# Scaling the second projections' outputs on ScalarE and adding them on GpSimd in a two-layer diffusion backbone

## The chip, the core and the metric

The kernel runs on one core of a Trainium2 chip. Its metric is the device time of one execution in microseconds (us), as the median of several runs. The engines are called by their names or, in rows of the profile, by short ones: PE is TensorE (PEld its weight loads), DVE VectorE, ACT ScalarE, POOL GpSimd, SP SyncE. Matmuls write to PSUM, which the kernel uses as eight banks of 512 float32 columns; everything else that is computed lives in SBUF. GpSimd does not appear in the kernel as a reader of PSUM: what it adds must first be in SBUF.

## The reference

512 latent tokens (`x`) and 256 context tokens (`ctx`) of width 1024 pass two layers. Each layer has three sub-layers: a SwiGLU feed-forward of inner width 2816 that counts half, a mixer (a short gated convolution in the first layer, attention in the second), and another half feed-forward. Every sub-layer has an RMSNorm, a shift and a scale, and a gate on its output, all three made from the conditioning vectors:

```python
h = norm_modulate(x_lat, norm_g[i, 0], m_lat[:, 0, 0], m_lat[:, 0, 1])
x_lat = x_lat + MACARON_WEIGHT * m_lat[:, 0, 2] * swiglu(h, ffn_w_in[i, 0], ffn_w_out[i, 0])

def swiglu(h, w_in, w_out):
    gate, up = jnp.split(h @ w_in, 2, axis=-1)
    return (jax.nn.silu(gate) * up) @ w_out
```

The vectors `m_lat` and `m_ctx` are `silu(c) @ ada_w + ada_b` for the latent and the context tokens. The context is carried as far as the attention reads it. The output is the latent stream after a last RMSNorm. What the change touches is the second product, `... @ w_out`, its gate and its addition to the stream.

## The kernel before

**Layout.** The stream of both kinds of tokens is one SBUF tile, `x_all`, of 8 chunks of 128 features with 768 tokens each: columns 0 to 511 latent, 512 to 767 context. Weights come by DMA as float32 (`raw`, five buffers) and are split into a high and a low half (`split`, lines 189 and 190): ScalarE rounds to the high one, VectorE subtracts for the low one. A product is then three matmuls (`mm3`, lines 861 to 863: high by high, high by low, low by high). Split weights go to eight tiles called `w`, filled ahead of TensorE; a tile is free again when TensorE has used it.

**Sub-layers.** They are named by layer and place: f00 (first feed-forward of the first layer), c01 (convolution), f02, f10, the attention, f12. In a feed-forward, `products` makes the first projection for 22 chunks of 128 inner features. The first two or three chunks are made directly, the others by seven half-size products M1 to M7 (`PRODUCTS`), whose operands are sums of quarters of the weights (lines 373 and 382, VectorE) and of the activations. Each product has a bank of PSUM under the tags A (three banks), C (three), B (one); ScalarE and VectorE take the results out (lines 1135 to 1212).

**Parts.** As soon as the chunks of a part are made, `out_steps` runs the second projection for them: `FFN_PARTS` is (2, 4, 4, 4, 4, 4), so a feed-forward has six parts, the first of two chunks, the others of four; the convolution has two. A part loops over the eight output chunks three at a time (3, 3, 2) and, for each, over the two token groups: 512 latent columns, then 256 context columns. A group takes three banks from A and C (`out_banks`), 12 matmuls of a bank in a part of four chunks. Then its eviction, line 929: VectorE reads the bank, multiplies it by the gate `gat` (a column of a tile) and adds the piece of the stream, in place. The last part of a sub-layer goes other ways: `out_close` (line 998) in f00, c01 and f02, `out_last` (line 1606) in f12, and in f10 `out_steps` itself with `after` set, which squares and norms the stream at once. The attention's output and f12 have one token group alone.

**Order.** TensorE's and SyncE's instructions keep the program's order. VectorE's, ScalarE's and GpSimd's are put in order by a scheduler that works with costs of its own; on the chip every engine works its queue in that order. In some stretches (the opening, the turn from one sub-layer to the next) the program's order holds for VectorE and ScalarE too.

**Work in the background.** The conditioning products run on VectorE in the shadow of the matmuls: `ada_step` (line 530) multiplies a 128 x 512 tile of `ada_w`, called `aw`, by `silu_row` and sums it, once for the latent and once for the context vector. `bg` and `bg_run` pace the steps over the products and the parts. The tiles `aw` are loaded by GpSimd's queue (`ada_next`, line 509) into four buffers in f00, two in c01, five in f02 and f10; each step asks for the load of the tile that many steps ahead, whose buffer that same step has just read.

**Small tiles.** The pool `tmp` has four tiles with the tag "t" of 512 columns, used in turn for squares, roots and the convolution's mixed rows; in the parts that the change touches they stand mostly unused.

Of the kernel before, what the change touches and what calls it, by code (L numbers as in the profile page):

```python
# [10 lines left out]
F32 = mybir.dt.float32  # L11
F32R = mybir.dt.float32r
BF16 = mybir.dt.bfloat16
AF = mybir.ActivationFunctionType
ALU = mybir.AluOpType
# [3 lines left out]
P = 128  # L19
# [4 lines left out]
NL = 512  # L24
# [54 lines left out]
def segments(off, n):  # L79

    out = []
    if off < NL:
        out.append((LAT, off, min(off + n, NL) - off))
    if off + n > NL:
        out.append((CTX, max(off, NL), off + n - max(off, NL)))
    return out
# [43 lines left out]
def backbone(ctx: ExitStack, tc: tile.TileContext, a: dict, out: bass.AP):  # L130
    nc = tc.nc
    act, dve, pe = nc.scalar, nc.vector, nc.tensor
# [3 lines left out]
    tmp = ctx.enter_context(tc.tile_pool(name="tmp", bufs=4))  # L136
    wp = ctx.enter_context(tc.tile_pool(name="wp", bufs=3))

    def ctile(name, shape, dt=F32):
        return const.tile(shape, dt, name=name, tag=name)  # L140
# [13 lines left out]
    def ptile(name, shape=(P, 512)):  # L154
        pool, tag = bank[name]
        return pool.tile(list(shape), F32, name=f"ps_{name}", tag=tag)
# [25 lines left out]
    gat = ctile("gat", [P, KC, 2])  # L182
# [108 lines left out]
    def w_get(most=1 << 30):  # L291
        w_fill(max(most, state["used"] + 1 - state["next"]))
        where, dst = ready[state["used"]]
        ready[state["used"]] = None
        state["used"] += 1
        taken.append(where)
        return dst
# [3 lines left out]
    def w_ahead(n):  # L301

        return w_get(max(0, state["used"] + 1 + n - state["next"]))

    def w_done():

        for where in taken:
            if where is None:
                state["open"] -= 1
            elif where[0] == "slot":  # L310
                state["extra"] -= 1
        taken.clear()
# [188 lines left out]
    ada_chunks, ada_loaded, ahead = [], {}, {}  # L501
    silu_row = {}

    def ada_next(n):

        if n < ahead["limit"]:
            t, kh, j = ada_chunks[n]
            w = ada_loaded[n] = ahead["pool"].tile([P, 512], F32, name=f"aw{t}_{kh}_{j}", tag="aw", bufs=ahead["depth"])
            nc.gpsimd.dma_start(w, a["ada_t"][t, kh, j])  # L509
# [12 lines left out]
    def ada_step(n, i, hm, nv):  # L522

        t, kh, j = ada_chunks[n]
        w = ada_loaded.pop(n)
        col = 4 * (hm % 2) + j
        for v in range(nv):
            total = mods[i][:, hm // 2, col, v : v + 1]
            junk = ptile("S")
            ins = dve.tensor_tensor_reduce(out=junk, in0=w, in1=silu_row[kh][:, v, :], scale=1.0, scalar=total if kh else ada_b[:, i, hm // 2, col : col + 1], op0=ALU.mult, op1=ALU.add, accum_out=total)  # L530
            tc.keep_in_program_order(ins)
        ada_next(n + ahead["depth"])
        if kh and j == 3:
            ada_done.add((i, hm))

    def ada_list():


        tasks = [(i, hm) for i in range(2) for hm in range(18) if i or hm > 5]
        at = 0  # L540
        for key, end in ADA_BY.items():
            steps = []
            for kh in range(2):
                steps += [lambda kh=kh: silu_load(kh)] + [rest] * 3
                for t in range(at, end):
                    i, hm = tasks[t]
                    for j in range(4):
                        steps.append(lambda n=len(ada_chunks), i=i, hm=hm: ada_step(n, i, hm, mod_groups(i, hm // 2)))
                        ada_chunks.append((t, kh, j))
            ada_tasks.extend((at, go) for go in steps)  # L550
            at = end
# [23 lines left out]
    def bg_run(share):  # L575
        if pace["n"] < pace["first"] or pace["done"] == pace["steps"]:
            return
        pace["used"] += share
        due = min(pace["steps"], int(np.ceil(pace["steps"] * pace["used"] / pace["room"] - 1e-6)))
        while pace["done"] < due:  # L580
            ada_tasks.pop(0)[1]()
            pace["done"] += 1
# [14 lines left out]
    def xs(m, off, n):  # L597
        return x_all[:, m, off : off + n]

    def sq_add(m, grp):  # L600
        off, n = grp
        if m == 0 and off == 0:
            ssq[:] = [stage["ssq"]()]
        if m == 0:
            act.activation(ssq[0][:, off : off + n], xs(m, off, n), AF.Square)
        else:
            sq_sum(sq_of(m, grp), grp)
# [11 lines left out]
    def preload_ln_exp():  # L619
        tc.keep_in_program_order(act.preload_act_table_set(LN_EXP))  # L620
# [39 lines left out]
    def norm_parts(grp):  # L660
        off, n = grp
        return parts_of(ssq[0][:, off : off + n], n, D)
# [62 lines left out]
    def in_order():  # L725

        region.append(ExitStack())
        region[0].enter_context(tc.manual_schedule(engines=BOOT_ORDERED))

    def free_order():  # L730
        region.pop().close()
# [128 lines left out]
    def mm3(ps, wh, wl, xh, xl, first, last, **kw):  # L860
        pe.matmul(ps, wh, xh, start=first, stop=False, **kw)  # L861
        pe.matmul(ps, wh, xl, start=False, stop=False, **kw)  # L862
        pe.matmul(ps, wl, xh, start=False, stop=last, **kw)  # L863
# [45 lines left out]
    def out_steps(groups, passes, gh, gl, npart, after, alloc, width, scarce=0):  # L909

        def run(grp, ms, units, major, tags=None):
            off, n = grp
            ps = [ptile(t) for t in tags] if tags else alloc(grp, len(ms))
            todo = [(f, u) for f in range(npart) for u in range(len(ms))] if major else [(f, u) for u in range(len(ms)) for f in range(npart)]
            for q, (f, u) in enumerate(todo):
                wh, wl = units[u]  # L920
                mm3(ps[u][:, :n], wh[:, f, :], wl[:, f, :], gh[f][:, off : off + n], gl[f][:, off : off + n], f == 0, f == npart - 1)
                if q % npart == npart - 1:
                    bg_run(OUT_SHARE * n / NT)
            if gates:
                gates.pop()()
            for m, p in zip(ms, ps):
                for v, o, w in segments(off, n):
                    x = xs(m, o, w)
                    dve.scalar_tensor_tensor(out=x, in0=p[:, o - off : o - off + w], scalar=gat[:, m, v : v + 1], in1=x, op0=ALU.mult, op1=ALU.add)  # L929

        held = []
        major = width == 3
        for m0 in range(0, KC, width):
            ms = range(m0, min(m0 + width, KC))
            units = [w_ahead(scarce) if scarce else w_get() for _ in ms]
            if after:
                run(passes[0], ms, units, major)
                held.append((ms, units))
                for m in ms:
                    sq_add(m, passes[0])  # L940
                if m0 < KC // 2 <= m0 + width:
                    preload_ln_exp()
                if ms[-1] < 6:
                    w_done()
                yield
            else:
                for grp in groups:
                    run(grp, ms, units, major)
                    major = False
                    yield  # L950
                w_done()
            major = False
        if after:
            in_order()
            steps = iter(after(passes[0], norm_parts(passes[0])))
            flat = [(m, u) for ms, units in held for m, u in zip(ms, units)]
            n2 = 1 if width == 3 else 2
            behind = PASS_STEPS[n2]
            for j in range(0, KC, n2):
                ms, units = zip(*flat[j : j + n2])  # L960
                run(passes[1], ms, units, False, LAST_BANKS[j : j + n2] if n2 == 1 else None)
                for what, n in behind.get(j, ()):
                    if what == "norm":
                        for _ in range(n):
                            for step in [next(steps, None)]:
                                if step:
                                    step()
                    else:
                        for m in n:
                            sq_add(m, passes[1])  # L970
            for step in steps:
                step()
            w_done()
            held_tiles.clear()
            pending.extend(after(passes[1], norm_parts(passes[1])))
            free_order()
# [724 lines left out]
    with tc.tile_pool(name="apool", bufs=1) as apool, tc.tile_pool(name="g0", bufs=1) as gp, tc.tile_pool(name="qp", bufs=1) as qp, psum(A=3, B=1, C=3, S=1):  # L1701
# [24 lines left out]
        with tc.tile_pool(name="boot", bufs=1) as bp, aw_pool():  # L1726
            in_order()
            op = opening(0, 0)
# [71 lines left out]
            op1 = opening(0, 1)  # L1800
# [94 lines left out]
```

## Time and profile before

| what | us |
|---|---|
| median of 3 runs | 2407.13 |
| lowest and highest run | 2406.97, 2408.5 |
| span of the profiled execution | 2405.2 |

The span goes from the first to the last instruction of one execution taken by the profiler; the runs' times are of other executions. A group's row gives its line, engine, operation, what it writes and reads, the shapes (partitions by elements) and the count, then busy time and the mean of one in ns, then how long the engine sat idle just before these instructions and who ended that. A row of stretches gives the stretch, its length, busy time and number of instructions of each engine in turn, the granted TensorE clock (1.00 is full), the busy share of the DMA engines and GB/s. A row of waits says who waited for whom: total, times, longest. A row of the timeline begins with start and duration. A busy matmul is one in flight, and neighbours overlap, so the step from one start to the next tells the pace.

### The profile page before, as it was taken

The numbers are of one execution on the slowest core, as the hardware profiler recorded it, in microseconds if no ns is written. First come the engines' busy times: TensorE is split into PE (matmuls) and PEld (weight loads), VectorE is DVE, ScalarE is ACT, GpSimd is POOL, SyncE is SP. The second block draws the span as 40 slices with busy tenths as digits, with TensorE's granted clock in tenths as the row PEclk, the third lists the DMA queues.
The fourth block names the chain that finished last, engine by engine and source line by source line (L and its number), as shares of the span: only waits on it lengthen the run. The fifth ranks groups of instructions, "written<-read, shape, count | busy, mean of one in ns | idle before, by whom it ended". The sixth has DMA issues, their size and how long they took to land.

```text
span 2405.2 us, 37639 instructions
## 1 busy us (share of the span) xinstructions
PE 2383.8 (99%) x14303; PEld 2258.6 (94%) x14303; DVE 2033.0 (85%) x4018; ACT 1164.8 (48%) x2198; POOL 135.2 (6%) x256
## 2 busy tenths in 40 slices
PE   8999999999999999999999999999999999999998
PEld 6999999999999999999999999999998889999998
DVE  6989989978988888888887988888778987987787
ACT  5634334355535653433435543343355776555555
POOL 0001111100000001000000001101100000000000
PEclk9999999999999999999999999999999999999999
DMA  9234444430334123323432144443441101133331
GB/s 334 87 112 137 130 126 129 131 115 27 106 106 132 33 69 115 127 93 119 126 100 73 49 124 126 146 136 122 141 131 45 53 10 58 67 110 102 106 106 62
DMA packets 93062, 253.71 MB, mean 105 GB/s; under 512 B 10320, under 2 KB 18640, under 8 KB 92880
## 3 DMA queue, kind: packets, MB, share of 16 engines
q1 hardware_dynamic: 71984, 183.65, 23.5%
q0 software_dynamic: 20352, 67.12, 9.4%
q8 instruction: 112, 1.84, 0.3%
q14 instruction: 70, 0.57, 0.1%
q10 hardware_dynamic: 544, 0.52, 0.1%
HBM read 249.16 MB, written 2.10 MB: 104 GB/s over the span
## 4 chain that ended last, share of the span: by engine, by line
PE 92%; DVE 3%; ACT 2%; DMA 1%; issue 1%; SPq 0%; DVEq 0%; ACTq 0%
PE ps_A L861 16%; PE ps_A L862 16%; PE ps_A L863 16%; PE ps_C L862 11%; PE ps_C L861 11%; PE ps_C L863 11%; PE ps_B L863 3%; PE ps_B L861 3%; PE ps_B L862 3%; PE ps_T L1542 1%; DMA ada<-in_ada_w 1%; ACT pr L1525 0%; DMA raw<-in_ffn_w_in 0%; DVE w L190 0%; PE ps_O L861 0%
## 5 line engine op out<-in xcount | busy, mean ns | idle before, releaser
L189 ACT ACTIVATE w<-raw 128x512 fp32r<-128x512 f32 (+1 forms) x862 | 522.4, 619 | 721.0 <-PE ps_A L863 229.7
L190 DVE TENSOR_TENSOR w<-raw,w 128x512 fp32r<-128x512 f32 (+1 forms) x862 | 574.3, 679 | 119.7 <-ACT w L189 105.8
L509 POOL DMA_DIRECT2D aw<-in_ada_t x240 | 129.1, 538 | 1374.8 <-DVE mods L530 973.9
L373 DVE TENSOR_TENSOR raw<-raw,raw 128x512 f32<-128x512 f32 x264 | 181.5, 689 | 9.0 <-DMA raw<-in_ffn_w_in 4.9
L862 PE MATMUL ps_C<-gl,w 128*128 128x512 f32 (+1 forms) x548 | 188.5, 344 | 0.0
L861 PE MATMUL ps_C<-gh,w 128*128 128x512 f32 (+1 forms) x548 | 188.4, 344 | 0.0
L863 PE MATMUL ps_C<-gh,w 128*128 128x512 f32 (+1 forms) x548 | 188.2, 343 | 0.0
L861 PE MATMUL ps_A<-gh,w 128*128 128x512 f32 (+1 forms) x540 | 185.8, 344 | 0.6 <-DVE x L929 0.6
L862 PE MATMUL ps_A<-gl,w 128*128 128x512 f32 (+1 forms) x540 | 185.7, 344 | 0.0
L863 PE MATMUL ps_A<-gh,w 128*128 128x512 f32 (+1 forms) x540 | 185.5, 344 | 0.0
L530 DVE CUSTOM_DVE_ANT_0 ps_S<-aw,silu_row,packed 128x512 f32<-128x512 f32 x208 | 156.9, 754 | 2.4 <-DMA aw<-in_ada_t 1.0
L530 DVE CUSTOM_DVE_ANT_0 ps_S<-aw,silu_row,mods 128x512 f32<-128x512 f32 x208 | 156.8, 754 | 1.0
L929 DVE SCALAR_TENSOR_TENSOR x<-ps_C,gat,x 128x512 f32<-128x512 f32 (+1 forms) x158 | 99.5, 631 | 43.1 <-PE ps_C L863 42.7
L861 PE MATMUL ps_A<-tB11h,w 128*128 128x384 f32 (+1 forms) x400 | 130.8, 327 | 0.2 <-ACT tB11h L785 0.2
L862 PE MATMUL ps_A<-tB11l,w 128*128 128x384 f32 (+1 forms) x400 | 130.3, 326 | 0.2 <-DVE tB11l L786 0.2
L863 PE MATMUL ps_A<-tB11h,w 128*128 128x384 f32 (+1 forms) x400 | 130.4, 326 | 0.0
L862 PE MATMUL ps_C<-tB22l,w 128*128 128x384 f32 (+2 forms) x376 | 121.8, 324 | 0.0
L863 PE MATMUL ps_C<-tB22h,w 128*128 128x384 f32 (+2 forms) x376 | 121.7, 324 | 0.0
L861 PE MATMUL ps_C<-tB22h,w 128*128 128x384 f32 (+2 forms) x376 | 121.5, 323 | 0.0
L929 DVE SCALAR_TENSOR_TENSOR x<-ps_A,gat,x 128x512 f32<-128x512 f32 (+1 forms) x162 | 101.8, 637 | 17.0 <-PE ps_A L863 16.7
L863 PEld LDWEIGHTS ps_C<-gh,w 128*128 128x128 f32 x548 | 103.9, 190 | 12.3
L861 PEld LDWEIGHTS ps_A<-gh,w 128*128 128x128 f32 x540 | 102.4, 190 | 14.0 <-issue 1.0
(486 smaller groups left out, 6946.0 us busy)
## 6 DMA issues: line engine op xcount, KB each, us to landing
raw<-in_ffn_w_in SPq DMA_DIRECT2D x170, 512.0 KB, 3.7
aw<-in_ada_t POOLq DMA_DIRECT2D x240, 256.0 KB, 3.0
raw<-in_ffn_w_out SPq DMA_DIRECT2D x80, 512.0 KB, 4.1
raw<-in_conv_w_in SPq DMA_DIRECT2D x24, 512.0 KB, 3.7
ada<-in_ada_w SPq DMA_DIRECT2D x28, 256.0 KB, 5.7
raw<-in_attn_w_qkv SPq DMA_DIRECT2D x12, 512.0 KB, 4.9
raw<-in_ada_w SPq DMA_DIRECT2D x8, 512.0 KB, 6.8
silu_row<-in_crow POOLq DMA_DIRECT2D x8, 512.0 KB, 4.2
```

The costliest lines, as they stand in the source:

```text
L189: hi = act.activation(dsth, src, AF.Copy)
L190: lo = dve.tensor_tensor(out=dstl, in0=src, in1=dsth.bitcast(F32), op=ALU.subtract)
L373: dve.tensor_tensor(out=quad(o), in0=quad(x), in1=quad(y), op=ALU.subtract)
L509: nc.gpsimd.dma_start(w, a["ada_t"][t, kh, j])
L530: ins = dve.tensor_tensor_reduce(out=junk, in0=w, in1=silu_row[kh][:, v, :], scale=1.0, scalar=total if kh else ada_b[:, i, hm // 2, col : ...
L861: pe.matmul(ps, wh, xh, start=first, stop=False, **kw)
L862: pe.matmul(ps, wh, xl, start=False, stop=False, **kw)
L863: pe.matmul(ps, wl, xh, start=False, stop=last, **kw)
L929: dve.scalar_tensor_tensor(out=x, in0=p[:, o - off : o - off + w], scalar=gat[:, m, v : v + 1], in1=x, op0=ALU.mult, op1=ALU.add)
L1542: pe.transpose(pt[:, c, :], pr[:, (c0 + c) * P : (c0 + c + 1) * P], ident)
```

## The change

Two places. In `out_steps`, an eviction of a part that is neither a sub-layer's last (`after` unset) nor of one token group alone is now two instructions: ScalarE's activation Copy reads the bank, multiplies by the gate and writes a `tmp` tile "t" named `oy`; GpSimd adds that tile to the stream, in place. The bank is free when ScalarE has read it, the tile when GpSimd has added it. Other evictions stay as they were. In `ada_step`, the load that a step asks for is that of the step before it: after step n it is tile n - 1 + depth, not n + depth; the first step of a sub-layer asks for none. The buffer that a load fills is the one that step n - 1 has read.

```diff
@@ ada_step
-        ada_next(n + ahead["depth"])
+        if n > ahead["start"]:
+            ada_next(n - 1 + ahead["depth"])
@@ out_steps, run
                 for v, o, w in segments(off, n):
                     x = xs(m, o, w)
-                    dve.scalar_tensor_tensor(out=x, in0=p[:, o - off : o - off + w], scalar=gat[:, m, v : v + 1], in1=x, op0=ALU.mult, op1=ALU.add)
+                    if after or len(groups) == 1:
+                        dve.scalar_tensor_tensor(out=x, in0=p[:, o - off : o - off + w], scalar=gat[:, m, v : v + 1], in1=x, op0=ALU.mult, op1=ALU.add)
+                    else:
+                        y = tmp.tile([P, NL], F32, name="oy", tag="t")[:, :w]
+                        act.activation(y, p[:, o - off : o - off + w], AF.Copy, scale=gat[:, m, v : v + 1])
+                        nc.gpsimd.tensor_tensor(out=x, in0=x, in1=y, op=ALU.add)
```

## The prediction

> **What bounds the kernel now.** I read the page first, then the busy time by stretches, then the list of what TensorE waited for, and last the timeline, because a busy TensorE need not be one at its peak. The first row is the span; in the second each engine has its busy time, its share and its number of instructions.
>
> ```profile
> span 2405.2 us, 37639 instructions
> PE 2383.8 (99%) x14303; PEld 2258.6 (94%) x14303; DVE 2033.0 (85%) x4018; ACT 1164.8 (48%) x2198; POOL 135.2 (6%) x256
> ```
>
> The parts that the change touches end between 76 and 1790 us. The next fence cuts the span there; behind the length of a stretch stand the busy times of TensorE, its weight loads, VectorE, ScalarE and GpSimd. Below is all that TensorE waited for in the middle stretch.
>
> ```profile
> 0.00:76.00 76.00, 69.54 (x381) 50.54 (x382) 52.66 (x106) 48.60 (x86) 3.54 (x11) 1.00 0.84 296
> 76.00:1790.00 1714.00, 1713.19 (x9808) 1655.93 (x9807) 1473.56 (x2928) 748.42 (x1371) 130.68 (x243) 1.00 0.35 109
> 1790.00:2405.20 615.20, 601.04 (x4117) 552.10 (x4116) 506.80 (x986) 367.80 (x742) 0.98 (x2) 1.00 0.22 72
> ```
>
> ```profile
> PE ps_A L861 <- DVE x L929: 0.6, 1, 0.6
> ```
>
> TensorE is idle for 1714.00 - 1713.19 = 0.81 us of the 1714 us, 0.6 of it in one wait for an eviction of the very line that is changed. The clock granted is 1.00 throughout. It remains that matmuls might run closer together than they do. The timeline shows them under a busy VectorE (an ada step, 170.15 to 170.90) and under an idle one (the last row: idle for 1.82 us before 936.64).
>
> ```profile
> 170.15 0.75 DVE L530 CUSTOM_DVE_ANT_0 ps_S<-aw,silu_row,packed 128x512 f32<-128x512 f32 x1
> 170.63 0.39 PE L862 MATMUL ps_C<-gl,w 128*128 128x512 f32 x1
> 170.86 0.39 PE L863 MATMUL ps_C<-gh,w 128*128 128x512 f32 x1
> ...
> 935.31 0.39 PE L862 MATMUL ps_C<-gl,w 128*128 128x512 f32 x1
> 935.53 0.39 PE L863 MATMUL ps_C<-gh,w 128*128 128x512 f32 x1
> ...
> 936.64 0.75 DVE L929 SCALAR_TENSOR_TENSOR x<-ps_C,gat,x 128x512 f32<-128x512 f32 x1 [1.82 <-PE ps_C L863]
> ```
>
> The step from one 512-column matmul to the next is 0.23 us in the first case and 0.22 in the second. Relieving VectorE does not quicken it. So the kernel is bound by TensorE's own stream, and what the change can win in its stretch is 0.81 us.
>
> **The change part by part.** The evictions in question are those of line 929:
>
> ```profile
> L929 DVE SCALAR_TENSOR_TENSOR x<-ps_A,gat,x 128x512 f32<-128x512 f32 x95 | 69.8, 748 | 15.6 <-PE ps_A L863 15.4
> L929 DVE SCALAR_TENSOR_TENSOR x<-ps_C,gat,x 128x512 f32<-128x512 f32 x89 | 66.6, 748 | 42.9 <-PE ps_C L863 42.7
> L929 DVE SCALAR_TENSOR_TENSOR x<-ps_C,gat,x 128x256 f32<-128x256 f32 x69 | 32.9, 480 | 0.2
> L929 DVE SCALAR_TENSOR_TENSOR x<-ps_A,gat,x 128x256 f32<-128x256 f32 x67 | 32.2, 480 | 1.3 <-PE ps_A L863 1.3
> ```
>
> Of these 184 + 136, 56 + 8 stay: those with one token group alone (40 in f12, 8 in the attention) and the last part of f10 (8 + 8). 128 of each form move: 16 parts (five of f00, f02 and f10, one of c01) with 8 + 8 each.
>
> VectorE loses 8 x (0.748 + 0.480) = 9.8 us a part, 157 us in all. ScalarE's and GpSimd's new instructions are not in the trace; these rows are nearest:
>
> ```profile
> L1135 ACT ACTIVATE g<-ps_A 128x256 f32<-128x256 f32 x20 | 7.6, 381 | 8.8 <-PE ps_A L863 8.8
> L1398 ACT ACTIVATE hs<-ps_A 128x512 f32<-128x512 f32 x6 | 3.5, 588 | 0.1
> L189 ACT ACTIVATE gh<-g 128x384 fp32r<-128x384 f32 x118 | 61.9, 524 | 44.8 <-DVE g L1212 36.8 <-DVE g L1204 8.0
> L1289 ACT ACTIVATE cy<-u,packed 128x384 f32<-128x384 f32 x8 | 4.9, 612 | 2.1 <-DVE u L1308 2.0
> masks.py:199 POOL TENSOR_SCALAR_AFFINE_SELECT ident<-ident 128x128 f32<-128x128 f32 x1 | 0.8, 772 | 0.1
> masks.py:199 POOL TENSOR_SCALAR_AFFINE_SELECT identb<-identb 128x128 f32<-128x128 f32 x1 | 0.3, 292 | 0.1
> L190 DVE TENSOR_TENSOR w<-raw,w 128x512 fp32r<-128x512 f32 x830 | 562.2, 689 | 119.7 <-ACT w L189 105.8
> ```
>
> ScalarE reads 512 columns of PSUM in 0.588 us and 256 in 0.381; a scale that is a column of a tile costs 0.612 - 0.524 = 0.088 more (third and fourth row). So 8 x (0.676 + 0.469) = 9.2 us a part, at least 7.8 without that surcharge, at most the 9.8 that VectorE needs now. GpSimd adds two SBUF tensors. Below it stands VectorE's own two-input instruction, 0.689 us for 512 columns, half of that for 256; above it the slower of GpSimd's two selects, 0.772 for 128 columns, which makes 3.1 and 1.5. I take the faster select (0.292), 1.17 and 0.58, because it is nearer to the VectorE row for the same work and the same operation stands in both selects. That is 8 x 1.75 = 14.0 us a part (8.3 to 37), beside the DMA issues. Now the cover, in parts of f00, f00's products, f02's first part, and another part of f02:
>
> ```profile
> 832.00:857.00 25.00, 24.89 (x143) 22.64 (x142) 24.81 (x45) 10.96 (x20) 0.00 (x0) 1.00 0.22 74
> 915.00:951.00 36.00, 36.00 (x209) 32.21 (x208) 32.16 (x71) 6.59 (x12) 4.84 (x9) 1.00 0.37 110
> 154.00:188.00 34.00, 34.00 (x198) 30.34 (x198) 33.23 (x78) 5.93 (x10) 5.92 (x11) 1.00 0.40 113
> 188.00:246.00 58.00, 58.00 (x333) 57.87 (x332) 52.56 (x109) 29.09 (x54) 5.91 (x11) 1.00 0.44 144
> ```
>
> ScalarE goes from 5.93 to 15.1 of 34 us, and in the short part from 10.96 to 20.2 of 25. GpSimd goes from 5.92 to 19.9 of 34. VectorE falls from 33.23 to 23.4. None is full, so all of this lies beside TensorE's work: I cost it at nothing. A new wait is ScalarE's, for the end of a group's matmuls; behind it in ScalarE's order stand splits of weights. What they are early by shows in what ScalarE waits for between 915 and 951 us:
>
> ```profile
> ACT w L189 <- PE ps_C L863: 12.0, 5, 7.2
> ACT w L189 <- PE ps_A L863: 6.6, 2, 5.8
> ```
>
> It waits up to 7.2 us for TensorE to give a weight tile back: all eight tiles are filled ahead, so a split that comes some us later finds its cover. Another new wait is for one of the four tmp tiles "t", which GpSimd frees. GpSimd works in order, and an add can stand behind an ada load that waits for VectorE:
>
> ```profile
> POOL aw L509 <- DVE mods L530: 23.5, 8, 9.4
> ```
>
> That is of 154 to 188 us; the longest of eight waits is 9.4 us. Four tiles hold an extra group of three, and a bank is asked for again one group pair later: 36 matmuls of 512 columns at 0.23 us and 36 of 256, at half of that, 12.4 us. So a delay of 9.4 us ends before the bank is wanted. Cost nothing; a delay 1 us beyond that in each of 16 parts would make 16 us, 2422.5.
>
> The load itself is moved one step back in the program, but the buffer that it fills is given free by the same step as before, so VectorE's wait for it need not change.
>
> ```profile
> aw<-in_ada_t POOLq DMA_DIRECT2D x240, 256.0 KB, 3.0
> ```
>
> Where adds hold the queue, a load lands late by their time, and VectorE waits up to 3.0 us. Only c01, with two buffers, is near that, and its weights are filled ahead too. Nothing again.
>
> The sum: the 0.6 us wait on line 929 goes, since that eviction stands behind VectorE's other work no longer; what is late next there is a split or ScalarE's own eviction, and the other 0.2 us of idle time stay. 2405.2 - 0.6 = 2404.6 us of span. The median of the runs, 2407.13, is 1.9 us above the profiled span, so 2406.5.
>
> **The rivals.**
>
> First, slower: GpSimd falls behind in the three parts of two chunks (f00, f02, f10). There the evictions come fastest, sixteen from 840.06 to 855.33, or 15.3 us:
>
> ```profile
> 840.06 0.74 DVE L929 SCALAR_TENSOR_TENSOR x<-ps_C,gat,x 128x512 f32<-128x512 f32 x1
> ...
> 855.33 0.48 DVE L929 SCALAR_TENSOR_TENSOR x<-ps_C,gat,x 128x256 f32<-128x256 f32 x1
> ```
>
> My 14.0 us just fits. If every add also waits out one VectorE instruction (0.689 us), an add takes 0.875 + 0.689 = 1.56 us and the part 25.0: GpSimd is 9.7 us late, the four tiles hold 4 x 1.56 = 6.2, and ScalarE, and then a bank, is held up to 3.5 us. Three parts give 10.5 us: 2417. It decides from where sixteen adds less four exceed 15.3 us, 1.28 us an add. For it: VectorE is busy 24.81 of 25 us there. Against it: the same stretch loses VectorE's evictions, and the idle group of banks may hold those 3.5 us.
>
> Second, slower: VectorE becomes the bound in f00. If it stands still during each add, a part and its products cost it 33.23 + 52.56 - 9.8 + 14.0 = 90.0 of 92 us. That fits; from 16 us of adds a part it does not. At 1.3 times my price (18.2) it lacks 2.2 us in each of four such rounds, 9 us: 2415.5. For it: most of VectorE's work there (ada steps, splits) reads two SBUF tensors. No row of this trace shows an add of GpSimd beside VectorE. The Trainium skill ("SBUF — State Buffer", section "Who interferes with whom") says that a VectorE instruction with two SBUF inputs and a GpSimd instruction that reads SBUF lock each other out, whichever begins first; that speaks against this change, and by it this rival and the one above both have their mechanism, at the prices given.
>
> Third, faster by more than a measurement can tell from no change (0.2%, 4.8 us): the changed queues shift the order of other work too, and the third stretch has 615.2 - 601.04 = 14.2 us of idle TensorE. A third of it gone would give 2402. Nothing in the change touches that stretch; the same shift could as well cost some.
>
> **How the numbers follow.** The forecast has 0.72: TensorE's stretch is full and every new instruction has cover. First rival 0.11, second 0.08, the longer wait in GpSimd's queue 0.03, third 0.06. Hence faster 0.06, same 0.72, slower 0.22. The time is the forecast's, 2406.5. Its own range is 2404 to 2410. The range for 8 in 10 reaches down to 2403.5, some 3 us for shifts of order, and up to 2416, over the second rival and most of the way to the first; about 0.15 is left out.
>
> **What would show it.** Line 929 with 64 instead of 320 instructions on VectorE; 256 new ones on ScalarE near 0.68 and 0.47 us, 256 on GpSimd near 1.17 and 0.58. TensorE between 76 and 1790 us idle for under 2 us, with its matmuls at the same steps. VectorE's busy time near 1876 us if nothing locks it; longer means of lines 190, 373 or 530 would show the lock. I am wrong if TensorE's waits name the new lines (ScalarE's eviction, or through it GpSimd's add) or splits of weights for several us in all, first at 90 to 110, 840 to 857 and 1352 to 1369 us.

## The result, and the profile after

The changed kernel takes 2480.81 us (median of 4 runs, 2478.99 to 2482.47) against 2407.05 for the kernel before on the same chip: ratio 1.0307, 95% interval 1.0295 to 1.032, so 74 us slower. The prediction said 2406.5, no change that could be measured.

The page of the changed kernel, its span and its engines' busy times (busy time, share of the span, number of instructions):

```profile
span 2479.8 us, 38129 instructions
PE 2408.4 (97%) x14303; PEld 2272.8 (92%) x14303; DVE 2122.0 (86%) x3762; ACT 1287.1 (52%) x2454; POOL 430.4 (17%) x512
```

The span grew by 2479.8 - 2405.2 = 74.6 us. TensorE has the same 14303 matmuls, yet is busy for 2408.4 - 2383.8 = 24.6 us longer: they ran slower. The other 50.0 us are idle time of TensorE. VectorE gave away 256 of its instructions, yet its busy time rose from 2033.0 to 2122.0 us.

What TensorE waited for, the first five rows (total, times, longest):

```profile
PE ps_C L862 <- ACT oy L934: 26.2, 7, 5.7
PE ps_A L862 <- DVE c L1152: 13.6, 11, 2.6
PE ps_A L862 <- ACT g L1149: 4.4, 2, 2.2
PE ps_C L484 <- DMA ada<-in_ada_w: 4.3, 1, 4.3
PE ps_A L863 <- DVE tT2l L190: 3.9, 1, 3.9
```

Up to line 531 both kernels number their lines alike; from there to the eviction this kernel's lines are those of before plus one, behind it plus six. The longest total is the new eviction (line 934), but VectorE's evictions of the products (line 1152) and its split of the activations (line 190) are there too. So it isn't one instruction that is late.

The groups of VectorE's and GpSimd's instructions, by shape (busy time, mean in ns, idle time before):

```profile
L190 DVE TENSOR_TENSOR w<-raw,w 128x512 fp32r<-128x512 f32 x830 | 615.3, 752 | 128.0 <-ACT w L189 115.3
L373 DVE TENSOR_TENSOR raw<-raw,raw 128x512 f32<-128x512 f32 x264 | 232.3, 881 | 23.1 <-DMA raw<-in_ffn_w_in 17.4
L530 DVE CUSTOM_DVE_ANT_0 ps_S<-aw,silu_row,mods 128x512 f32<-128x512 f32 x208 | 205.4, 987 | 3.6
L1157 DVE TENSOR_TENSOR g<-ps_C,g 128x384 f32<-128x384 f32 x68 | 37.7, 554 | 9.3 <-PE ps_C L864 9.3
L935 POOL TENSOR_TENSOR x<-x,oy 128x512 f32<-128x512 f32 x128 | 179.7, 1420 | 111.8 <-ACT oy L934 110.3
L935 POOL TENSOR_TENSOR x<-x,oy 128x256 f32<-128x256 f32 x128 | 116.2, 927 | 26.6 <-ACT oy L934 26.2
L934 ACT ACTIVATE oy<-ps_A,gat 128x512 f32<-128x512 f32 x63 | 43.0, 686 | 25.9 <-PE ps_A L864 25.9
L934 ACT ACTIVATE oy<-ps_A,gat 128x256 f32<-128x256 f32 x65 | 30.8, 474 | 31.4 <-PE ps_A L864 19.9 <-POOL x L935 11.5
```

The same groups of the kernel before:

```profile
L373 DVE TENSOR_TENSOR raw<-raw,raw 128x512 f32<-128x512 f32 x264 | 181.5, 689 | 9.0 <-DMA raw<-in_ffn_w_in 4.9 <-DMA raw<-in_conv_w_in 0.2
L530 DVE CUSTOM_DVE_ANT_0 ps_S<-aw,silu_row,mods 128x512 f32<-128x512 f32 x208 | 156.8, 754 | 1.0
L1151 DVE TENSOR_TENSOR g<-ps_C,g 128x384 f32<-128x384 f32 x68 | 37.8, 556 | 11.1 <-PE ps_C L863 11.1
```

The weights' low halves went from 689 to 752 ns, their sums from 689 to 881, the ada steps from 754 to 987: all read two SBUF operands. The evictions on line 1157 (1151 before), which read one operand from PSUM and one from SBUF, took 556 ns before and take 554 now, but that shows little: none of them ran beside an addition. The lengthening lies beside the new additions. Of the 264 weight sums (line 373), the 223 that met no addition took 691 ns in the median, and the 41 that met one took 1925 on average. This timeline of VectorE and then GpSimd shows one place (start, duration; the last row is three additions):

```profile
165.68 0.76 DVE L530 CUSTOM_DVE_ANT_0 ps_S<-aw,silu_row,packed 128x512 f32<-128x512 f32 x1
...
167.38 4.43 DVE L530 CUSTOM_DVE_ANT_0 ps_S<-aw,silu_row,packed 128x512 f32<-128x512 f32 x1
```

```profile
166.90 0.54 POOL L509 DMA_DIRECT2D aw<-in_ada_t  x1 [1.15 <-DVE mods L530]
167.45 3.80 POOL L935 TENSOR_TENSOR x<-x,oy 128x512 f32<-128x512 f32 x3
```

One ada step began 0.07 us before three additions and ended 0.56 us after the last of them: 4.43 us instead of 0.76, longer by 3.67, about the time of the additions. The additions had piled up behind an ada load that waited for VectorE.

Where it costs time is read by cutting both traces at the same matmuls: the part of two chunks in f00 (90 to 112 us before) and f00's four-chunk parts with their products (130 to 520 before). Each row has the stretch, its length, then TensorE, weight loads, VectorE, ScalarE and GpSimd, and the granted clock. First the kernel before, then the changed one:

```profile
90.00:112.00 22.00, 21.37 (x126) 19.51 (x125) 21.96 (x38) 9.81 (x19) 0.00 (x0) 1.00 0.16 50
130.00:520.00 390.00, 390.00 (x2240) 374.85 (x2239) 349.08 (x734) 152.14 (x280) 42.48 (x79) 1.00 0.42 129
```

```profile
89.52:117.28 27.76, 23.84 (x126) 21.90 (x125) 24.12 (x24) 18.15 (x36) 22.45 (x16) 0.88 0.12 39
135.31:559.40 424.09, 401.79 (x2240) 384.30 (x2239) 384.77 (x666) 181.26 (x344) 109.27 (x143) 0.97 0.39 118
```

The same 2240 matmuls take 424.09 us instead of 390.00, 34.1 us more: 22.3 us in which TensorE is idle and 11.8 in which it is busy for longer. VectorE has 68 instructions fewer and is busy for 35.7 us longer. The two-chunk part lost 5.8 us.

Why busy for longer: behind most of TensorE's stops of over 2 us the granted clock falls to half for a while. TensorE stopped from 190.37 to 195.18 us; around that the stretches read (the clock is the third figure from the end):

```profile
190.40:193.70 3.30, 0.00 (x0) 0.00 (x0) 3.27 (x4) 0.00 (x0) 2.09 (x4) 1.00 0.38 124
193.75:200.55 6.80, 5.37 (x21) 5.37 (x22) 6.47 (x11) 4.54 (x9) 2.72 (x3) 0.50 0.34 99
200.60:205.00 4.40, 4.40 (x27) 4.40 (x26) 4.33 (x8) 1.64 (x3) 2.41 (x3) 1.00 0.28 88
```

Half clock begins 3.4 us into the stop and lasts 6.8 us, 5.4 of them with TensorE at work. The Trainium skill ("TensorE: Matmul & The Clock Gate", Part 1) tells of a half-rate state after an idle window of about 3.4 us that is left again after a busy one; the 3.4 us of idle time before this fall agree. A shorter stop was enough, too: behind the one from 306.64 to 308.89 us (2.24 us) the clock is half from 309.80 to 313.21. It isn't always: three other stops of 2.2 to 2.3 us (before 914.53, 1438.04 and 1716.74 us) have no half clock behind them. In f00's stretch the half clock adds up to 23.9 us. Half of that, 11.9, is about the 11.8 us that TensorE is busy for longer.

### The profile page after: what moved, and what is told of

Its sections match the earlier page's. It is cut to its first block, busy times and chain, and to the rows that moved or that the text cites. A ratio compares the mean times of both kernels' runs of the same rounds, so it can differ in the third digit from the quotient of the medians.

```text
span 2479.8 us, 38129 instructions
## 1 busy us (share of the span) xinstructions
PE 2408.4 (97%) x14303; PEld 2272.8 (92%) x14303; DVE 2122.0 (86%) x3762; ACT 1287.1 (52%) x2454; POOL 430.4 (17%) x512
## 4 chain that ended last, share of the span: by engine, by line
PE 62%; DVE 16%; issue 16%; ACT 3%; DMA 2%; POOL 0%; SPq 0%; DVEq 0%; ACTq 0%; POOLq 0%
PE ps_A L862 11%; PE ps_A L863 11%; PE ps_A L864 11%; PE ps_C L862 7%; PE ps_C L863 7%; PE ps_C L864 7%; DVE w L190 5%; DVE ps_S L530 3%; DVE raw L373 3%; PE ps_B L864 2%; PE ps_B L862 2%; PE ps_B L863 2%; DMA raw<-in_ffn_w_in 1%; DVE mods L530 1%; ACT w L189 1%
## 5 line engine op out<-in xcount | busy, mean ns | idle before, releaser
L189 ACT ACTIVATE w<-raw 128x512 fp32r<-128x512 f32 (+1 forms) x862 | 521.5, 618 | 418.0 <-DVE raw L373 161.6
L190 DVE TENSOR_TENSOR w<-raw,w 128x512 fp32r<-128x512 f32 (+1 forms) x862 | 627.3, 739 | 128.0 <-ACT w L189 115.3
L935 POOL TENSOR_TENSOR x<-x,oy 128x256 f32<-128x256 f32 (+1 forms) x256 | 294.1, 1173 | 138.4 <-ACT oy L934 136.5
L373 DVE TENSOR_TENSOR raw<-raw,raw 128x512 f32<-128x512 f32 x264 | 232.3, 881 | 23.1 <-DMA raw<-in_ffn_w_in 17.4
L862 PE MATMUL ps_C<-gh,w 128*128 128x512 f32 (+1 forms) x548 | 192.9, 352 | 26.2 <-ACT oy L934 26.2
L530 DVE CUSTOM_DVE_ANT_0 ps_S<-aw,silu_row,mods 128x512 f32<-128x512 f32 x208 | 205.4, 987 | 3.6
L530 DVE CUSTOM_DVE_ANT_0 ps_S<-aw,silu_row,packed 128x512 f32<-128x512 f32 x208 | 199.3, 958 | 5.8 <-DMA aw<-in_ada_t 1.9
L864 PE MATMUL ps_C<-gh,w 128*128 128x512 f32 (+1 forms) x548 | 191.6, 350 | 0.0
L934 ACT ACTIVATE oy<-ps_C,gat 128x512 f32<-128x512 f32 (+1 forms) x128 | 74.2, 579 | 133.8 <-PE ps_C L864 129.0
L862 PE MATMUL ps_A<-tT4h,w 128*128 128x384 f32 (+1 forms) x352 | 116.3, 330 | 13.6 <-DVE c L1152 13.6
```

Of the source, the lines that this page charges most:

```text
L189: hi = act.activation(dsth, src, AF.Copy)
L190: lo = dve.tensor_tensor(out=dstl, in0=src, in1=dsth.bitcast(F32), op=ALU.subtract)
L373: dve.tensor_tensor(out=quad(o), in0=quad(x), in1=quad(y), op=ALU.subtract)
L934: act.activation(y, p[:, o - off : o - off + w], AF.Copy, scale=gat[:, m, v : v + 1])
L935: nc.gpsimd.tensor_tensor(out=x, in0=x, in1=y, op=ALU.add)
```

## The experiments

Each gives the median and the ratio to the kernel before on the same chip, 3 rounds. Two ideas stood against each other at first. Port: VectorE's two-operand instructions and GpSimd's additions shut each other out. Queue: ScalarE's evictions now stand behind its weight splits, which wait for VectorE, and that order alone costs the time. The moved ada load was a third suspect.

**The two edits apart.** The later ada load alone, in the kernel before:

```diff
-        ada_next(n + ahead["depth"])
+        if n > ahead["start"]:
+            ada_next(n - 1 + ahead["depth"])
```

> The kernel before with only the later ada load. Both theories, the port (VectorE and GpSimd shut each other out) and the queue (ScalarE's evictions stand behind splits that wait for VectorE), put none of the loss on the load: 2405 to 2409 us. A third, that the load one step later starves VectorE's ada steps, expects part of the 74 us, over 2415, and VectorE's waits for aw well over the 1.0 us of before.

2406.76 us, ratio 1.0001 (0.9992 to 1.001). And the change without it (the reverse diff in the changed kernel):

> The changed kernel with the ada load at its old step. Port and queue theories: as the changed kernel, 2470 to 2495. If the later load is what keeps GpSimd's adds from standing behind loads, it gets slower, over 2500; if the later load is itself a cost, faster, under 2465.

2476.85 us, 1.0296 (1.0279 to 1.0313). The load's place costs nothing in the kernel before, as predicted, and some 4 us at most in the changed one. The loss is the evictions'.

**What GpSimd does, at the same places.** First, ScalarE scales and VectorE adds:

```diff
-                        nc.gpsimd.tensor_tensor(out=x, in0=x, in1=y, op=ALU.add)
+                        dve.tensor_tensor(out=x, in0=x, in1=y, op=ALU.add)
```

> ScalarE scales as in the changed kernel, VectorE adds instead of GpSimd: the evictions keep their place on ScalarE, GpSimd adds nothing. VectorE has 16 x 8 x (0.689 + 0.42) = 142 us of adds in place of 157 us of evictions. Port theory: no instruction of VectorE is lengthened (line 530 at 0.754 us, line 373 at 0.689) and the kernel is back near 2407, at most 2415. Queue theory: ScalarE's evictions still wait behind splits that wait for VectorE, which is as full as before: 2430 to 2480.

2405.42 us, 0.9995 (0.9986 to 1.0005). ScalarE's new evictions and their order cost nothing while VectorE is in time. Next, GpSimd is as busy as with the additions, but reads nothing (the kernel leaves the second projections of these parts out of the stream):

```diff
-                        nc.gpsimd.tensor_tensor(out=x, in0=x, in1=y, op=ALU.add)
+                        for _ in range(3):
+                            nc.gpsimd.memset(y, 0.0)
```

> GpSimd's add is replaced by three fills of the tile oy, which wait for ScalarE and write SBUF but read nothing; the second projections of these parts are thus left out of the stream. Every queue and wait stays, only the read goes. Port theory, with the read as what collides: VectorE's instructions at their old lengths, 2405 to 2415. If a busy GpSimd or its queue (adds, loads, four tiles) is the cost whatever it does: over 2440. Queue theory: 2430 to 2480, since the order on ScalarE is the same.

2405.66 us, 0.9996 (0.9986 to 1.0005). Its groups:

```profile
L936 POOL MEMSET oy<- 128x256 f32 (+1 forms) x768 | 298.4, 427 | 130.5 <-ACT oy L934 118.1
L373 DVE TENSOR_TENSOR raw<-raw,raw 128x512 f32<-128x512 f32 x264 | 181.8, 689 | 8.1 <-DMA raw<-in_ffn_w_in 2.4
L530 DVE CUSTOM_DVE_ANT_0 ps_S<-aw,silu_row,mods 128x512 f32<-128x512 f32 x208 | 157.2, 756 | 3.5
```

298.4 us of GpSimd work, as much as the additions' 179.7 + 116.2, lengthen nothing. It isn't that GpSimd is busy, nor its queue. The four tiles are excluded for the four-chunk parts alone: in f00's two-chunk part the fills take GpSimd 17.7 us, the additions 22.5. Then GpSimd reads, but one operand only (the same projections are left out):

```diff
-                        nc.gpsimd.tensor_tensor(out=x, in0=x, in1=y, op=ALU.add)
+                        for _ in range(2):
+                            nc.gpsimd.tensor_copy(out=y, in_=x)
```

> The changed kernel in which GpSimd, in place of the addition, copies the stream's part into the tile twice, so it reads one SBUF operand and not two (the second projections of these parts are left out of the stream). If any read of SBUF by GpSimd shuts VectorE's two-operand instructions out: VectorE's sums and ada steps are lengthened as with the additions, and the time is 2440 us or more. If it takes two operands read at once: they keep 689 and 754 ns, and the time is 2406 us.

2425.56 us, 1.0078 (1.0063 to 1.0093): between the two expectations.

```profile
L936 POOL COPY oy<-x 128x256 f32<-128x256 f32 (+1 forms) x512 | 374.7, 758 | 121.7 <-ACT oy L934 112.0
L373 DVE TENSOR_TENSOR raw<-raw,raw 128x512 f32<-128x512 f32 x264 | 197.8, 750 | 16.5 <-DMA raw<-in_ffn_w_in 10.8
L530 DVE CUSTOM_DVE_ANT_0 ps_S<-aw,silu_row,mods 128x512 f32<-128x512 f32 x208 | 179.0, 860 | 3.6
```

VectorE's sums and steps are lengthened (750 and 860 ns), less than by the additions, although the copies keep GpSimd busy for longer (374.7 us against 295.9). So one SBUF operand on GpSimd's side is enough; why it costs less, no run tells. The lock is shown. The Trainium skill's rule ("SBUF — State Buffer", section "Who interferes with whom"), which the prediction cited, names two SBUF operands on VectorE's side, a read on GpSimd's, and no contention with a GpSimd instruction that only writes. The fills and the copies agree with the last two; the first is seen in side_adds below.

**From the lock to the time.** ScalarE's high halves no longer wait for VectorE's weight sums:

```diff
-                split(dh, dl, quad(2))
+                split(dh, dl, quad(2), early=quad(3))
```

(and so for the two other products; `split` takes the high half from `early`.)

> The changed kernel, in which ScalarE's high halves for the Strassen products M5, M6 and M3 are taken from the plain quadrant and not from VectorE's weight sum (so the sums are left out of those high halves; VectorE still does all its work, GpSimd all its additions). ScalarE's splits then no longer wait for VectorE's sums. Port theory by way of the queue (VectorE is lengthened by the additions, ScalarE's split waits for it, and the eviction stands behind that split): TensorE's waits for the new eviction and the half-clock time after them go, most of the 47 us that the four-chunk parts lost; 2430 to 2450 us. Port theory without the queue (VectorE's lateness reaches TensorE through its own tiles): within 10 us of 2481.

2492.21 us, 1.036 (1.0344 to 1.0375): even slower, so the first expectation fell; it is also some 1 us beyond the second (within 10 us of 2481). What TensorE waited for:

```profile
PE ps_A L862 <- DVE c L1152: 43.9, 12, 7.2
PE ps_C L862 <- ACT oy L934: 6.4, 3, 5.7
```

The wait for ScalarE's eviction is nearly gone and stands again at VectorE's own eviction. The name in the wait list was only the nearest link; by this the late engine is VectorE. The opposite test has the later ada load too, keeps the evictions on VectorE and lets GpSimd read beside it:

```diff
+                    if not after and len(groups) == 2:
+                        y = tmp.tile([P, NL], F32, name="oy", tag="t")[:, :w]
+                        nc.gpsimd.tensor_tensor(out=y, in0=x, in1=x, op=ALU.add)
```

> The kernel before, with its evictions on VectorE, and GpSimd beside it doubles a part of the residual stream into a spare tile at the places of the new additions (a result that nobody reads). Port theory: VectorE carries its old evictions and is lengthened as well, about 2030 + 246 us busy; it is slower than the changed kernel or like it, 2480 to 2560 us. Queue theory, in which the evictions on ScalarE are needed for the loss: under 2440 us. Cost of the evictions' new place alone, without a shared port: 2407 us.

2462.61 us, 1.0237 (1.0222 to 1.0252). Neither number was met, but it is well above 2440: 56 of the 74 us need no eviction on ScalarE. This run also shows what an operand in PSUM does:

```profile
L373 DVE TENSOR_TENSOR raw<-raw,raw 128x512 f32<-128x512 f32 x264 | 196.2, 744 | 13.8 <-DMA raw<-in_ffn_w_in 9.7
L930 DVE SCALAR_TENSOR_TENSOR x<-ps_A,gat,x 128x512 f32<-128x512 f32 x95 | 69.5, 745 | 8.9 <-PE ps_A L864 8.8
L930 DVE SCALAR_TENSOR_TENSOR x<-ps_C,gat,x 128x256 f32<-128x256 f32 x69 | 32.5, 473 | 0.0
```

VectorE's evictions, which read PSUM and one SBUF operand, kept their time (748 and 480 ns before), although 125 of the 320 ran beside an addition of GpSimd. The sums, with two SBUF operands, went from 689 to 744.

**By place.** No ada steps in the parts (`OUT_SHARE = 0` for 4), and the same in the kernel before as its control:

> The changed kernel with no ada steps run in the parts of the second projections (all of them run elsewhere). Port theory with the ada steps as what is lengthened most (754 to 987 ns each): the 34 us of the four-chunk parts of the first sub-layer and the 8.6 us of the attention sub-layer go for the most part, the 20 us of the two-chunk parts, where there are no ada steps to speak of, stay; 2425 to 2440 us. If the ada steps aren't the link: 2470 us or more.

> The kernel before with no ada steps run in the parts of the second projections: the control for the changed kernel with the same edit (2443 us). 2407 us within 3; if it is 2420 or more, that edit costs something by itself and the comparison has to take it off.

2442.89 us, 1.0155 (1.0138 to 1.0172), and 2419.47, 1.0053 (1.0038 to 1.0068). The control was needed: moving the ada steps costs 13 us by itself. Against it the change costs 2442.89 - 2419.47 = 23.4 us, not 74. f00's four-chunk parts, the control first, then the changed kernel:

```profile
129.58:528.93 399.35, 393.31 (x2239) 376.55 (x2239) 344.57 (x733) 151.66 (x280) 42.48 (x79) 0.99 0.39 126
```

```profile
135.84:535.87 400.03, 393.53 (x2240) 376.78 (x2240) 330.89 (x668) 185.28 (x345) 114.41 (x143) 0.99 0.40 125
```

With no ada steps beside them, all of GpSimd's additions cost 0.7 us here instead of 34.1. The two-chunk parts keep their loss, 19.7 us in all by the same cuts, and make up most of the 23.4. The change in four-chunk parts alone:

```diff
-                    if after or len(groups) == 1:
+                    if after or len(groups) == 1 or npart == 2:
```

> The change made in the four-chunk parts alone; the two-chunk parts keep VectorE's evictions. Port theory, additive by place: the 20 us of the two-chunk parts go, the rest stays; about 2461 us. If the two-chunk parts' delay is what makes the later parts late: under 2440 us.

2459.02 us, 1.0217 (1.0202 to 1.0232), as the additive count had it: the three two-chunk parts cost some 20 us. Every second addition on VectorE:

```diff
-                        nc.gpsimd.tensor_tensor(out=x, in0=x, in1=y, op=ALU.add)
+                        (dve if m % 2 else nc.gpsimd).tensor_tensor(out=x, in0=x, in1=y, op=ALU.add)
```

> The changed kernel with every second 128-row block's addition on VectorE and the others on GpSimd. VectorE's lateness counts only beyond the slack that TensorE's buffers give: less than half of the 74 us, 2412 to 2440 us. Every microsecond of collision costs the same: half, 2444 us.

2419.84 us, 1.0059 (1.0042 to 1.0076): half the additions cost 13 us, a sixth of the loss. The loss doesn't grow in proportion to the additions.

**VectorE late without GpSimd.** VectorE adds, and does useless work behind each addition:

```diff
-                        nc.gpsimd.tensor_tensor(out=x, in0=x, in1=y, op=ALU.add)
+                        dve.tensor_tensor(out=x, in0=x, in1=y, op=ALU.add)
+                        z = y[:, :256]
+                        dve.tensor_tensor(out=z, in0=z, in1=z, op=ALU.add)
```

> ScalarE scales, VectorE adds (no GpSimd additions at all), and behind each addition VectorE does one useless 128x256 addition on a tile of its own, about 0.42 us, 256 times, so that its busy time comes to that of the changed kernel (2020 + 108 = 2128 us against 2122). VectorE's lateness by itself is the cause, whoever makes it late: well above 2407, 2440 to 2490 us, with the same TensorE waits and half-clock stretches. Something else in GpSimd's additions, beside VectorE's time, is needed: 2405 to 2412 us.

2414.19 us, 1.0032 (1.002 to 1.0044), near the second expectation. That looked like a case against VectorE's lateness as the whole cause, and turned me to another theory: that it is the few long stand-stills that count. If each VectorE instruction's time over the median of its line and shape is added up, the changed kernel has 209 us of lengthening, 90 of them in 27 instructions that are over 2 us too long. Two kernels tested that. Additions with a memset behind each, in which VectorE can get in:

```diff
                         nc.gpsimd.tensor_tensor(out=x, in0=x, in1=y, op=ALU.add)
+                        nc.gpsimd.memset(y, 0.0)
```

> The changed kernel with one GpSimd memset of the tile behind each addition, about 0.4 us in which GpSimd does not read SBUF, so that VectorE can get in between two additions. Long stand-stills theory: the VectorE instructions lengthened by over 2 us (27 in the changed kernel) nearly vanish, the lengthening per addition stays under 1.3 us, and the time falls to 2410 to 2445 us although GpSimd is busy 100 us more. Sum theory (every microsecond of lengthening costs alike): 2481 times nothing saved but in proportion to the lengthening that is left, 2450 to 2481 us. GpSimd's own time as the bound: slower than 2481.

2468.07 us, 1.0256 (1.0239 to 1.0273). Of the 27, 8 are left, the longest ada step falls from 4590 to 3199 ns, yet the lengthening is still 201 us and the loss 61 us. And late_vector with the useless work in clumps of nine (`adds` starts as an empty list):

```diff
+                        adds.append(1)
+                        if len(adds) % 9 == 0:
+                            z = y[:, :256]
+                            for _ in range(9):
+                                dve.tensor_tensor(out=z, in0=z, in1=z, op=ALU.add)
```

> As late_vector (VectorE adds, and does useless 128x256 additions, 2414 us), but the useless additions come nine at a time behind every ninth addition: the same 108 us of VectorE time in 28 stand-stills of about 3.8 us instead of 256 of 0.42 us, and no GpSimd additions. Long stand-stills theory: 2425 to 2450 us, with half-clock stretches. Sum theory: 2411 to 2418 us, as late_vector.

2423.55 us, 1.0069 (1.0054 to 1.0084). Clumps cost 9 us more than the spread work, so long stand-stills do matter, but they aren't the main thing: that theory fell. The ada loads issued from SyncE, so that no addition piles up behind them, and their control:

```diff
-            nc.gpsimd.dma_start(w, a["ada_t"][t, kh, j])
+            nc.sync.dma_start(w, a["ada_t"][t, kh, j])
```

> The changed kernel with the ada loads issued from SyncE's queue and not from GpSimd's, so that no addition stands behind a load that waits for VectorE. If the additions come in runs because of that queue: fewer VectorE instructions lengthened by over 2 us in the four-chunk parts, and 2430 to 2460 us unless SyncE's weight loads now wait; the two-chunk parts keep their 20 us. If not: 2470 to 2490 us. Weight loads held up on SyncE would show in the control as well.

> The kernel before with the ada loads issued from SyncE's queue: control for ada_on_sp. 2407 us within 3 if SyncE's weight loads have room to wait; over 2415 if they haven't.

2456.11 us, 1.0206 (1.0191 to 1.0221), and 2407.12, 1.0002 (0.9993 to 1.0012). A third of the loss hangs on that queue: the longest runs of additions go, with 155 us of lengthening left.

What late_vector had lacked was dose. Its 256 useless instructions overlap their neighbours and add 68 us of VectorE time, not 108, so VectorE still fitted beside TensorE. Two and three of them behind each addition, as an edit of late_vector:

```diff
-                        dve.tensor_tensor(out=z, in0=z, in1=z, op=ALU.add)
+                        for _ in range(2):
+                            dve.tensor_tensor(out=z, in0=z, in1=z, op=ALU.add)
```

> As late_vector (VectorE adds, one useless 128x256 addition behind each; 2414 us), with two useless additions. They overlap one another a little: one behind each addition raised VectorE's busy time by 68 us in all, by about 4 us in a stretch of 85 us. Two make about 82 to 84, 86 to 88, 86 to 88 and 124 us in the stretches that TensorE does in 85, 85, 90 and 130, as in the changed kernel. Fullness theory (VectorE is the bound where its work no longer fits beside TensorE's, and only there): the loss is no longer 7.6 us but several times it, 2430 to 2470 us. If it takes GpSimd's additions: twice late_vector's 8.8 us above the same kernel without useless work, 2420 to 2426 us.

> The same with three useless additions, about 5 us more VectorE work in a stretch than with two. Fullness theory: VectorE's work is above TensorE's in nearly all four-chunk stretches, and each further microsecond costs one or more: 2480 to 2560 us. If it takes GpSimd's additions: 2428 to 2440 us.

2467.01 us, 1.0255 (1.0238 to 1.0272), and 2569.47, 1.0674 (1.0658 to 1.069): from 9 us over vector_add to 62 and then 164, with no addition on GpSimd. The third kernel is 9 us above its range (2480 to 2560). The same 2240 matmuls of f00 in vector_add, late_vector, and those with two and three (the columns as above; the one after TensorE's and its loads' is VectorE's busy time):

```profile
128.79:518.80 390.01, 390.01 (x2240) 374.82 (x2239) 347.83 (x733) 186.46 (x344) 42.51 (x79) 1.00 0.40 129
```

```profile
132.41:524.72 392.31, 391.17 (x2239) 374.70 (x2239) 363.33 (x797) 183.45 (x344) 42.52 (x79) 1.00 0.41 129
```

```profile
137.57:555.58 418.01, 399.15 (x2239) 382.69 (x2239) 385.79 (x861) 184.43 (x345) 42.59 (x79) 0.97 0.38 121
```

```profile
143.65:584.11 440.46, 400.85 (x2240) 383.69 (x2239) 406.99 (x925) 184.33 (x344) 42.58 (x79) 0.96 0.36 115
```

With 348 us of VectorE work the stretch keeps TensorE's 390; with 363 it takes 2.3 us more. At 385.8 it takes 418.0, and the changed kernel, at 384.8, takes 424.1. The other kernels, cut at the same matmuls, show that the stretch grows with VectorE's work. The two without ada steps in the parts are left out: their work is in another order, and their control alone takes 399.4.

| kernel | VectorE busy, us | stretch, us |
|---|---|---|
| fill_not_add | 328.4 | 390.0 |
| vector_add | 347.8 | 390.0 |
| before | 349.1 | 390.0 |
| copy_not_add | 359.2 | 395.3 |
| clumped_vector | 361.7 | 393.6 |
| late_vector | 363.3 | 392.3 |
| half_adds | 364.2 | 396.3 |
| ada_on_sp | 365.5 | 411.7 |
| side_adds | 377.1 | 414.3 |
| the change | 384.8 | 424.1 |
| late_vector_x2 | 385.8 | 418.0 |
| four_only | 385.8 | 422.0 |
| loose_sums | 386.3 | 430.4 |
| spaced_adds | 386.9 | 424.9 |
| late_vector_x3 | 407.0 | 440.5 |

Delay begins between 349 and 359 us. Near 386 us the stretches differ by up to 12.4 us, and the changed kernel takes 6.1 us more than late_vector_x2. So the same VectorE time without GpSimd makes 28.0 of the 34.1 us; where the rest comes from isn't shown. The one that stands off is ada_on_sp, some 18 us above its neighbours. Why, no run tells. VectorE isn't filled to 390 because it waits itself, for ScalarE's high halves and TensorE's results, some 25 us in this stretch of late_vector.

**What is left.** In c01 the same matmuls took 9.1 us more (170.00 to 179.10), where late_vector_x2, with more VectorE work there (151.0 us against 148.2), lost nothing. ScalarE's rows in the changed kernel:

```profile
718.75 1.06 ACT L515 ACTIVATE silu_row<-silu_row 128x1024 f32<-128x1024 f32 x1 [10.27 <-DMA silu_row<-in_crow]
719.72 0.67 ACT L934 ACTIVATE oy<-ps_C,gat 128x512 f32<-128x512 f32 x1
```

The eviction stands behind a SiLU on ScalarE that waited 10.27 us for a load out of GpSimd's queue, and that load was issued late, between additions. TensorE stood for 5.7 us and then ran at half clock. With the ada loads on SyncE's queue (ada_on_sp) the longest wait there is 1.7 us and the same matmuls take 172.1. This is the queue theory, true at one place; it is read from the traces and wasn't tried by itself. No version beat the kernel before by more than the measurement can tell.

## Why the prediction was wrong

- What bounds the kernel before, TensorE's stream, was right, and so were the later load at nothing and ScalarE's prices (0.676 and 0.469 us put down, 0.686 and 0.474 measured).
- GpSimd's price was too low, 1.17 and 0.58 us against 1.42 and 0.93: 18.8 us a part, not 14.0. In a run of three, where VectorE is the one that waits, the larger takes 3.80 / 3 = 1.27 us.
- The step that failed is "None is full, so all of this lies beside TensorE's work: I cost it at nothing". It took VectorE's evictions off and added nothing for the lock, though the rows of lines 190 and 373 showed two operands in SBUF. In f00's stretch VectorE goes from 349.1 to 328.4 us without the lock (fill_not_add) and to 384.8 with it. In the whole span these are 2033, 1929 and 2122 us: the lock costs VectorE 193. The 1876 us that the prediction named were too low even without it, since VectorE's instructions overlap one another and 157 us of them taken away save 104 of busy time.
- The second rival had the mechanism, VectorE as the bound in f00. Its condition was met: it decided from 16 us of additions a part, and there were 18.8. By its own formula that is 33.23 + 52.56 - 9.8 + 18.8 = 94.8 of 92 us, 2.8 us in each of four rounds, 11 us in all. Measured in that stretch: 34.1. Its sum for VectorE's work came out by luck: four times 18.8 - 9.8 is 36.0 us, and 35.7 were measured, but the evictions taken away saved 20.7 and not 39.2, and the lock cost 56.4 and not 75.2. Two other terms were mis-sized. VectorE was let fill all of TensorE's time, while delay begins between 349 and 359 of 390 us. And each stop of TensorE was counted once, while the clock behind it cost 11.8 us on top of 22.3. Nor was it confined to f00: the two-chunk parts of f02 and f10 lost some 7 us each.
- The first rival's condition was met as well (22.45 us for 16 additions in the two-chunk part, 1.40 each, over its 1.28). But late_vector_x2 makes the same part 27.5 us long with VectorE alone, and in the changed kernel TensorE's longest wait there, 3.9 us, was for VectorE's split. ScalarE did wait for tiles that GpSimd still held, 1.5 us in f00's part and 4.4 us in f02's and in f10's. In copy_not_add, where VectorE has only 16.1 us of work in f00's part and GpSimd's copies take 25.9, about 14 of the loss of 19 us lie at the two-chunk parts. So this rival may well have a share of the 20 us that the change loses at them; how large, no run tells.
- ScalarE's new wait was looked at from one side. The prediction asked what the splits behind an eviction would suffer, not what an eviction suffers behind a split that waits for VectorE: there TensorE waited 26.2 us. vector_add shows that this order is harmless as long as VectorE is in time.
- The chance for the second rival, 0.08, was too small: the Trainium skill's rule and the operands in the rows spoke for its mechanism, and "no row of this trace shows an add of GpSimd beside VectorE" left only its price open.

## What to carry to other kernels

Before moving elementwise work from VectorE to GpSimd, look at what VectorE does at that time. Here its other instructions read two operands from SBUF, and it got 193 us of waiting for 104 us of work given away. Test an engine's room by stretches and not by its share of the span, and leave it time for its own waits; here that was some 8 to 10% of a stretch. When TensorE's wait list names an engine, ask what that engine was waiting for: here ScalarE was named, and VectorE was late.

## What was not expected of the hardware

GpSimd kept VectorE out not for one addition but for runs of them: 4.43 us for an ada step of 0.76 beside three additions of 3.80 us together, although by the trace the step had begun before them. In other places the two took turns: two 128x768 additions of VectorE took 4.03 us instead of 1.82 between GpSimd's. What decides which of the two happens, no run tells. A memset between additions cut the longest such step to 3.20 us. At one place a stop of TensorE of 2.24 us was enough for half clock behind it, at three others stops of nearly that length were not.
